# Hybrid attention, Fourier and Hyena block on one core: square sums, filters and modulation loads of the first phase rearranged

## The chip, the core and the metric

The kernel runs on one core of a Trainium2 chip. The metric is the device time of one execution in microseconds (us). In the text PE is TensorE, DVE is VectorE, ACT is ScalarE, and SP is SyncE, which here only issues DMAs. "L157" is line 157 of the kernel before.

## What is computed

One layer of a diffusion backbone over 256 latent tokens and 256 context tokens of width 2048. Cut to what matters here:

```
s_lat, s_ctx = silu(c), silu(c_ctx)
mod   = s_lat @ ada_w + ada_b           # six parts of 2048: sh1, sc1, g1, sh2, sc2, g2
mod_c = s_ctx @ ada_w + ada_b
h  = rmsnorm(x,   norm1_g) * (1 + sc1)  + sh1
hc = rmsnorm(ctx, norm1_g) * (1 + csc1) + csh1
q, k, v, f, hy = split(h @ w_in)
kc, vc = split(hc @ w_in[:, 1024:3072])
a = neighbourhood attention of q over k, v and all of kc, vc
y = concat(rmsnorm(a), rmsnorm(fourier(f)), rmsnorm(hyena(hy, filters)))
x = x + g1 * (y @ w_out)
x = x + g2 * mlp(modulated rmsnorm(x))
return rmsnorm(x)
```

The Hyena filters come from a small network of two sine layers over 256 positions: `hdn = sin(freq * (sin(freq * (z @ w1 + b1)) @ w2 + b2))`, `h = (hdn @ w3) * decay`, with a forward and a backward half for each of two orders. What the later stages need of them is a spectrum of the sum and one of the difference of the two halves; the backward half has no element 0.

## The kernel before

Everything is float32. The large products run as three float32r products (high by high, high by low, low by high; `mm3`, L159), so every weight chunk that arrives is split by ACT (`w_hi`, L168) and DVE (`w_lo`, L169). Products whose operands are plain float32 appear in the trace as two PE instructions each.

**First phase (L344 to L584).** It computes the keys and values of both streams, `kT` and `v_t`. The 16 row tiles of the model width are taken in five blocks of 2, 2, 4, 4 and 4 (`blocks`). A block has four column groups (`group`, L502): two for the keys, in which a latent and a context half follow each other, and two for the values. The first block writes its sums by ACT, the later ones add by DVE (L527).

A block needs its row tiles normalised and modulated, `hprep` (L474). That needs `A1` and `B1`, the modulation columns, which come from `ada_w`: a block of 2 row tiles takes 4 MB of it, one of 4 takes 8 MB, in loads of 512 KB (`ada_load`, L425). `part` (L435) loads all that one of the two halves (scale `m=0`, shift `m=1`) needs, multiplies it with the two silu vectors on PE (L445, four strips of 32 columns side by side), copies the result (L447), transposes it (L165) and reduces it (L451). The two parts of block b+1 are placed in the program before the groups 0 and 2 of block b; those of block 0 (`p0`, `p1`) and of block 1 (`e`, `e`) stand in the start.

**The start** is an order of named steps written out by hand, `start` in `CFG` (L52), each name a step of the dictionary at L545. In the order of the string: constants are loaded (`hp`, `pk`, `h3`, `dc`, `ft`), then the latent tokens (`x0 x1`); `si` is the silu; `w0` to `w3` are PE products whose results nobody reads (`warm`, L376); `n1s`, `n2s` are the sine layers (`sine`, L364); `hw` forms sum and difference of the filter weights on 64 rows (L384); `fr` computes element 0 apart (L388); `f0 f1` are the filters, `s0 s1` their spectra (`fold`, L171). The squares of the tokens (`squares`, L411) are taken by ACT, summed over four row tiles at a time by DVE (L418, `TENSOR_REDUCE`), and the four partial sums are summed over the rows by PE with columns of one element (`rms_bcast`, L197), which then puts the factor on all 128 rows through a diagonal matrix (`dg`, L208). `sr` loads and silus `s_row`, the vector that the side work reads.

**Side work.** Four further modulation vectors are computed by DVE from 128 loads of 512 KB (`ada_col_t`, L308, L309), two per `pump` (L318). `p1` in `CFG` gives the pumps in each block of the first phase.

**What sets the order.** SP issues all loads in the order of the program, and an issue waits until its buffer is free. Weight chunks, `ada_w` loads and side loads share one pool of 8 buffers of 512 KB (`w_raw`). On the other engines the framework orders the instructions when the kernel is built, by the program's order and by its own forecast of when operands are there; on the chip each engine then runs its list in order.

After the first phase come the Fourier and Hyena groups with their projections (L670 to L760), attention with the output projection, and the gated MLP. Nothing of them is touched.

Of the kernel before, what the change touches and what calls it, by code (L numbers as in the profile page):

```python
# [15 lines left out]
P = 128  # L16
D = 2048
# [18 lines left out]
for _n, _k in V_LAYOUT:  # L36
# [10 lines left out]
    p1=(3, 0, 3, 5, 6),  # L47
# [4 lines left out]
    start='hp pk h3 dc ft x0 x1 si w0 n1s w1 n2s hw w2 w3 a00 a01 a10 fr q0 f0 p0 a11 p1 n0 h0 s0 c0 w c1 f1 e s1 q1 n1 h1 sr e',  # L52
    late='',
    warm=(8, 2, 6, 3),
# [70 lines left out]
def hybrid_block(ctx: ExitStack, tc: tile.TileContext, a: dict, out: bass.AP):  # L125
# [71 lines left out]
    def rms_bcast(pool_, sqs, n, name):  # L197
        ps = bank()
        for t in range(2):
            for j, sq in enumerate(sqs):  # L200
                mm(ps[:, t : t + 1], sq[:, t * P : (t + 1) * P], ones[:, 0:1], j == 0, j == len(sqs) - 1)
        ms = pool_.tile([P, 2], F32, name=f"{name}_m", tag=f"{name}_m")
        TS(ms[:], ps[:, 0:2], 1.0 / n, EPS, op0=ALU.mult, op1=ALU.add)
        r = rstd_of(pool_, ms[:], 2, name)
        ps = bank()
        for t in range(2):
            dg = cst.tile([P, P], F32, tag="dg", name="dg", bufs=2)
            TS(dg[:], ident, r[:, t : t + 1], None, op0=ALU.mult)  # L208
# [3 lines left out]
        return rb  # L212

# [13 lines left out]
    class Weights:  # L227
        def __init__(self, stack, nraw, nsp, side=None):
            self.raw = pool(stack, "w_raw", nraw, side)
            self.sp = pool(stack, "w_split", nsp, side)  # L230

        def load(self, src, nk, n):
            r = self.raw.tile([P, nk, n], F32, tag="raw", name="raw")
            nc.sync.dma_start(r[:], src.rearrange("p (k n) -> p k n", n=n))
            return r

        def chunk(self, src, i, nk, n):
            raws = []
            for q in range(2):
                z = (slice(None), slice(q * nk // 2, (q + 1) * nk // 2))  # L240
                raws.append((z, self.load(src[2 * i + q], nk // 2, n)))
            hi = self.sp.tile([P, nk, n], F32R, tag="hi", name="w_hi")
# [86 lines left out]
    c_pool = pool(p1s, "c_lo", 1, "right")  # L329
    s_t = p1.tile([P, KT, 32], F32, name="s_t")  # L330
# [13 lines left out]
    if True:  # L344
        hpack = w1.raw.tile([64, L + 2 * 64 + 3], F32, tag="raw", name="hpack")
        hw3, hwsd = spec[:64, 0], spec[:64, 1]
        tb = v_t[:, :, HYW:]
        decay = tb[:, 0:2, :]
        kz = p1.tile([P, 4, HYW], F32, name="kz")
        hv = hpack[:, 0:3]  # L350
        hw1 = hpack[:33, 3:67]
        hw2 = hpack[:, 67:131]
        zT = hpack[:33, 131 : 131 + L]
        hd1, hd2 = tb[:64, 2, :L], tb[:64, 2, L:]
# [9 lines left out]
        def sine(dst, w, src, b):  # L364
            ps = bank()
            mm(ps[:64, :L], w, src, True, True)
            arg, k = tb[:64, 3, :L], tb[:64, 3, L:]
            TS(arg, ps[:64, :L], hv[:, b : b + 1], hv[:, 2:3], op0=ALU.add, op1=ALU.mult)
# [12 lines left out]
        def sums():  # L381
            for o in range(2):
                for z, op in enumerate((ALU.add, ALU.subtract)):
                    TT(hwsd[:, 2 * o + z, :], hw3[:, 2 * o, :], hw3[:, 2 * o + 1, :], op=op)  # L384

        frow = p1.tile([1, 2, HYW], F32, name="frow")

        def first_row(o):  # L388
            ps = bank()
            mm(ps[0:1, :], hd2[:, 0:1], hw3[:, 2 * o, :], True, True)  # L390
            TT(frow[:, o, :], ps[0:1, :], decay[0:1, 0, :], op=ALU.mult)
# [14 lines left out]
    if True:  # L406
# [4 lines left out]
        def squares(v):  # L411
            parts = []
            for q in range(4):
                pt = v_t[:, q, v * L : (v + 1) * L]
                sq = kT[:, 2 * (q % 2) : 2 * (q % 2) + 2, :].rearrange("p a (b n) -> p a b n", n=L)
                for j in range(2):
                    nc.scalar.activation(sq[:, j], xs[v].tiles[2 * q + j][:], AF.Square)
                nc.vector.tensor_reduce(pt, sq.rearrange("p a b n -> p n (a b)"), axis=AX.X, op=ALU.add)  # L418
                parts.append(pt)
            return parts  # L420

        def normalise(v, parts):
            rbs[v] = rms_bcast(p1, parts, D, f"rs{v}")

        def ada_load(k0, w, m, q):  # L425
            n2 = 2048 // w
            nh = n2 // 2
            return [w1.load(a["ada_t"][ada_at[k0, m, 2 * q + i]], nh, w) for i in range(2)]

        def prep_pieces(k0, nk):  # L430
# [4 lines left out]
            def part(m):  # L435
                raws = []
                for q in range(KT // n2):
                    raws += ada_raw.pop((m, q)) if (m, q) in ada_raw and k0 == 0 else ada_load(k0, w, m, q)
                if m == 0:
                    st_["red"] = p1.tile([P, 2, 4, 2], F32, tag="red", name="red", bufs=2)  # L440
                red = st_["red"]
                ps = bank()
                for kt in range(KT):
                    j = kt % 4
                    nc.tensor.matmul(ps[32 * j : 32 * j + 32, :w], s_t[:, kt, :], raws[kt // (n2 // 2)][:, kt % (n2 // 2), :], start=kt < 4, stop=kt >= KT - 4, skip_group_check=True)  # L445
                sb = p1.tile([P, 512], F32, tag="adasb", name="adasb", bufs=1)
                nc.scalar.copy(sb[:, :w], ps[:, :w])  # L447
                ps = bank()
                for i in range(nk):
                    transpose(ps[:, i * P : (i + 1) * P], sb[:, i * P : (i + 1) * P])  # L450
                nc.vector.tensor_reduce(red[:, m, :nk, :], ps[:, :w].rearrange("p (i j m) -> p i m j", j=4, m=32)[:, :, 0:2, :], axis=AX.X, op=ALU.add)  # L451

            def first():
                part(0)

            def second():
                part(1)
                red = st_["red"]
                for vv in range(2):
                    TT(red[:, 0, :nk, vv], red[:, 0, :nk, vv], vec[:, V_B0 + 16 + k0 : V_B0 + 16 + k0 + nk], op=ALU.add)  # L460
                    STT(A1[:, k0 : k0 + nk, vv], red[:, 0, :nk, vv], 1.0, vec[:, V_N1 + k0 : V_N1 + k0 + nk], op0=ALU.add, op1=ALU.mult)
                    TT(B1[:, k0 : k0 + nk, vv], red[:, 1, :nk, vv], vec[:, V_B0 + k0 : V_B0 + k0 + nk], op=ALU.add)
                if k0 > 0:
                    hprep(k0, nk, 0)
                    hprep(k0, nk, 1)

            return [first, second]
# [62 lines left out]
        pieces = block_pieces(0)  # L530
        parts = {}
        ahead = block_pieces(1)
# [4 lines left out]
        def first_rows():  # L537
            first_row(0)
            first_row(1)

        def sq(v):
            parts[v] = squares(v)

        wn = CFG["warm"]
        steps = {  # L545
            "hp": lambda: nc.sync.dma_start(hpack[:], a["hpack"]),
            "pk": lambda: nc.sync.dma_start(pack[:], a["pack"]),
            "h3": lambda: nc.sync.dma_start(hw3, a["hy_w3"][0].rearrange("k (g n) -> k g n", n=HYW)),
# [3 lines left out]
            "sr": silu_row, "si": silu, "n1s": lambda: sine(hd1, hw1, zT, 0), "n2s": lambda: sine(hd2, hw2, hd1, 1), "hw": sums,  # L552
            "w0": lambda: warm(ones[:], wn[0]), "w1": lambda: warm(decay[:, 0, :], wn[1]),
            "w2": lambda: warm(ftab.rearrange("p a n -> p (a n)"), wn[2]), "w3": lambda: warm(xs[0][:, 0, :], wn[3]),
            "c0": lambda: load_pairs(xs[1], a["cT"], 0), "c1": lambda: load_pairs(xs[1], a["cT"], 1),
            "fr": first_rows, "f0": lambda: filters(0), "f1": lambda: filters(1), "s0": lambda: spectra(0), "s1": lambda: spectra(1),
            "q0": lambda: sq(0), "q1": lambda: sq(1), "n0": lambda: normalise(0, parts[0]), "n1": lambda: normalise(1, parts[1]),
            "a00": lambda: pre_ada(0, 0), "a01": lambda: pre_ada(0, 1), "a10": lambda: pre_ada(1, 0), "a11": lambda: pre_ada(1, 1),
            "p0": pieces[0], "p1": pieces[1],
# [4 lines left out]
        late = CFG["late"].split()  # L564
        for z in CFG["start"].split():
            steps[z]()
        for b in range(len(blocks)):
            todo = (ahead if b == 0 else block_pieces(b + 1)) if b + 1 < len(blocks) else []
            n0 = len(todo)
            budget = 0.0  # L570
            for g in range(4):
# [3 lines left out]
                while late and b == 0:  # L575
                    z = late.pop(0)
                    if z == "|":
                        break
                    steps[z]()
# [319 lines left out]
def laid_out(inp):  # L899
# [28 lines left out]
    h = np.zeros((64, L + 2 * 64 + 3), f32)  # L928
    for i, n in enumerate(("hy_b1", "hy_b2", "hy_freq")):
        h[:, i] = inp[n][0]  # L930
    h[:33, 3:67] = inp["hy_w1"][0]
    h[:, 67:131] = inp["hy_w2"][0]
    h[:33, 131:] = z.T
# [49 lines left out]
```

## Time and profile before

| what | us |
|---|---|
| median of 3 runs (1346.88 to 1348.91) | 1347.93 |
| the profiled execution, whole | 1349.0 |
| its span, first to last instruction | 1347.2 |
| PE busy in the span | 1315.8 |
| DVE busy | 906.1 |
| ACT busy | 555.9 |

The page shows busy time by engine, the span in 40 slices, the DMA queues, the chain of work that ended last, and the costliest groups of instructions. PE's granted clock over the whole span is 0.991. The loads moved 309.35 MB. A row of the windows view has, for one stretch, its length, then busy time and number of instructions of PE, PE's weight loads, DVE, ACT and, where it ran, POOL, and at last the granted PE clock, the busy share of the DMA engines, and GB/s.

### The profile page before, as it was taken

The numbers are of one execution on the slowest core, as the hardware profiler recorded it, in microseconds if no ns is written. First come the engines' busy times: TensorE is split into PE (matmuls) and PEld (weight loads), VectorE is DVE, ScalarE is ACT, GpSimd is POOL, SyncE is SP. The second block draws the span as 40 slices with busy tenths as digits, with TensorE's granted clock in tenths as the row PEclk, the third lists the DMA queues.
The fourth block names the chain that finished last, engine by engine and source line by source line (L and its number), as shares of the span: only waits on it lengthen the run. The fifth ranks groups of instructions, "written<-read, shape, count | busy, mean of one in ns | idle before, by whom it ended". The sixth has DMA issues, their size and how long they took to land.

```text
span 1347.2 us, 24475 instructions
## 1 busy us (share of the span) xinstructions
PE 1315.8 (98%) x10262; PEld 1232.1 (91%) x10262; DVE 906.1 (67%) x1320; ACT 555.9 (41%) x738; POOL 0.9 (0%) x7
## 2 busy tenths in 40 slices
PE   8899999999999999989999999999999999999996
PEld 4486887999989889989999999999999999999996
DVE  5855668957999889976676767644446555654653
ACT  3542313133343665445443444333334444443542
POOL 0000000000000000000000000000000000000000
PEclk9899999999999999989999999999999999999998
DMA  8788687888669865846777777855555555555541
GB/s 321 281 324 304 241 338 291 323 253 286 212 249 330 309 197 180 281 136 211 252 251 247 250 250 239 281 195 186 184 188 184 189 186 189 187 187 187 182 151 63
DMA packets 93039, 313.05 MB, mean 232 GB/s; under 512 B 16000, under 2 KB 16192, under 8 KB 92480
## 3 DMA queue, kind: packets, MB, share of 16 engines
q1 hardware_dynamic: 92928, 311.49, 67.4%
q8 instruction: 80, 1.31, 0.4%
q14 instruction: 31, 0.25, 0.1%
HBM read 309.35 MB, written 2.10 MB: 231 GB/s over the span
## 4 chain that ended last, share of the span: by engine, by line
PE 94%; DVE 3%; ACT 1%; DMA 1%; issue 0%; DVEq 0%; ACTq 0%; POOL 0%; POOLq 0%
PE acc_ps L157 87%; PE mi_ps L157 4%; PE mi_ps L445 2%; PE mi_ps L165 1%; DMA raw<-in_ada_t 1%; DVE raw L309 0%; ACT w_hi L168 0%; DVE w_lo L169 0%; DMA raw<-in_ada_col_t 0%; DVE xr L894 0%; ACT L188 0%; DVE Y L717 0%; ACT kz L176 0%; ACT s_row L362 0%; DVE u L645 0%
## 5 line engine op out<-in xcount | busy, mean ns | idle before, releaser
L169 DVE TENSOR_TENSOR w_lo<-raw,w_hi 128x1024 fp32r<-128x1024 f32 x376 | 447.9, 1220 | 247.2 <-ACT w_hi L168 246.2
L168 ACT CAST w_hi<-raw 128x1024 fp32r<-128x1024 f32 x376 | 380.4, 1048 | 527.4 <-PE acc_ps L157 475.1
L157 PE MATMUL acc_ps<-h_hi,w_hi 128*128 128x256 f32 x1408 | 395.3, 281 | 1.6 <-ACT h_hi L224 1.6
L157 PE MATMUL acc_ps<-h_hi,w_lo 128*128 128x256 f32 x1408 | 395.3, 281 | 0.0
L157 PE MATMUL acc_ps<-h_lo,w_hi 128*128 128x256 f32 x1408 | 395.3, 281 | 0.0
L157 PEld LDWEIGHTS acc_ps<-h_hi,w_hi 128*128 128x128 f32 x1408 | 265.8, 189 | 1.9 <-ACT h_hi L224 1.9
L157 PEld LDWEIGHTS acc_ps<-h_lo,w_hi 128*128 128x128 f32 x1408 | 265.9, 189 | 0.0
L157 PEld LDWEIGHTS acc_ps<-h_hi,w_lo 128*128 128x128 f32 x1408 | 265.8, 189 | 0.0
L157 PE MATMUL acc_ps<-yh,w_hi 128*128 128x256 f32 x704 | 196.9, 280 | 0.0
L157 PE MATMUL acc_ps<-yl,w_hi 128*128 128x256 f32 x704 | 196.8, 280 | 0.0
L157 PE MATMUL acc_ps<-yh,w_lo 128*128 128x256 f32 x704 | 196.5, 279 | 0.0
L309 DVE SCALAR_TENSOR_TENSOR raw<-raw,s_row 128x1024 f32<-128x1024 f32 x128 | 154.1, 1217 | 30.5 <-DMA raw<-in_ada_col_t 30.5
L157 PE MATMUL acc_ps<-hx_hi,w_hi 128*128 128x256 f32 x512 | 145.1, 284 | 0.0
L157 PE MATMUL acc_ps<-hx_lo,w_hi 128*128 128x256 f32 x512 | 144.4, 282 | 0.0
L157 PE MATMUL acc_ps<-hx_hi,w_lo 128*128 128x256 f32 x512 | 144.0, 283 | 0.0
L157 PEld LDWEIGHTS acc_ps<-yh,w_hi 128*128 128x128 f32 x704 | 132.3, 188 | 0.0
L157 PEld LDWEIGHTS acc_ps<-yh,w_lo 128*128 128x128 f32 x704 | 132.1, 188 | 0.0
L157 PEld LDWEIGHTS acc_ps<-yl,w_hi 128*128 128x128 f32 x704 | 131.9, 187 | 0.0
L157 PEld LDWEIGHTS acc_ps<-hx_hi,w_hi 128*128 128x128 f32 x512 | 96.6, 189 | 5.0 <-issue 4.8
L157 PEld LDWEIGHTS acc_ps<-hx_hi,w_lo 128*128 128x128 f32 x512 | 96.2, 188 | 2.9 <-issue 2.9
L157 PEld LDWEIGHTS acc_ps<-hx_lo,w_hi 128*128 128x128 f32 x512 | 96.5, 188 | 0.8 <-issue 0.7
L623 DVE SCALAR_TENSOR_TENSOR xr<-acc_ps,G,xr 128x256 f32<-128x256 f32 x64 | 27.2, 477 | 20.8 <-PE acc_ps L157 20.8
(222 smaller groups left out, 1546.7 us busy)
## 6 DMA issues: line engine op xcount, KB each, us to landing
raw<-in_ffn_t SPq DMA_DIRECT2D x264, 512.0 KB, 4.3
raw<-in_ada_col_t SPq DMA_DIRECT2D x128, 512.0 KB, 4.8
raw<-in_ada_t SPq DMA_DIRECT2D x64, 512.0 KB, 6.5
raw<-in_w_in_t SPq DMA_DIRECT2D x48, 512.0 KB, 5.3
raw<-in_w_kv_t SPq DMA_DIRECT2D x32, 512.0 KB, 4.5
raw<-in_w_out_t SPq DMA_DIRECT2D x32, 512.0 KB, 4.7
x_in<-in_xT SPq DMA_DIRECT2D x8, 256.0 KB, 6.9
x_in<-in_cT SPq DMA_DIRECT2D x8, 256.0 KB, 8.0
```

What stands on the lines that cost most here:

```text
L157: nc.tensor.matmul(ps, lhsT, rhs, start=start, stop=stop, skip_group_check=True)
L165: nc.tensor.transpose(ps, src, ident[:n, :n])
L168: nc.scalar.copy(hi, src)
L169: TT(lo, src, hi.bitcast(F32), op=ALU.subtract)
L309: STT(r, r, 1.0, s_row[:, h * NA : (h + 1) * NA], op0=ALU.mult, op1=ALU.mult, accum_out=sums_[:, f, h : h + 1])
L445: nc.tensor.matmul(ps[32 * j : 32 * j + 32, :w], s_t[:, kt, :], raws[kt // (n2 // 2)][:, kt % (n2 // 2), :], start=kt < 4, stop=kt >= KT - ...
L623: STT(xr[:, c, :], pss[nt // 2][:, (nt % 2) * L : (nt % 2 + 1) * L], cols[:, c : c + 1], xr[:, c, :], op0=ALU.mult, op1=ALU.add)
```

## The change

- **Tokens first, two queues.** `hpack` and `pack` are issued by ACT, the latent tokens are SP's first loads, then `h3 dc ft`, half of block 0's modulation loads (`a00 a01`), the context tokens (`c0 c1`), the first weight chunk (`W`, `load_early`), and the other half (`a10 a11`).
- **Square sums on PE.** ACT squares each tile pair as before; PE sums them over the rows, for the latent tokens with a matrix of ones, so that the sum stands on all rows and the factor is worked out there (`rms_rows`), for the context tokens with columns of one element (`col_sums`).
- **Filters over 128 rows.** The second sine layer is computed twice, on rows 0 to 63 and 64 to 127, so that forward and backward weights stand below each other; sum and difference come from the products themselves, with a copy of the layer whose lower half has the sign turned (`signed`). `sums` and `first_row` go; `kz` moves into a part of `v_t`.
- **Pieces of 1 MB.** `part` becomes `piece`: one product over 1 MB of `ada_w`, 4 pieces for a block of 2 row tiles, 8 for one of 4, spread over the four groups of the block before. Three of eight loads go to a new pool of 3 buffers (`a_raw`). Block 1's pieces move out of the start into block 0.
- **Moved.** `s_row` is loaded and silued in block 1. The pumps are 0, 0, 2, 6, 9 in place of 3, 0, 3, 5, 6. Two kinds of unread products are left (`wm`, 8 of 128 columns; `wp`, 3 of 384).

```diff
-    p1=(3, 0, 3, 5, 6),
+    p1=(0, 0, 2, 6, 9),
-    start='hp pk h3 dc ft x0 x1 si w0 n1s w1 n2s hw w2 w3 a00 a01 a10 fr q0 f0 p0 a11 p1 n0 h0 s0 c0 w c1 f1 e s1 q1 n1 h1 sr e',
-    warm=(8, 2, 6, 3),
+    start='hp pk x0 x1 h3 dc ft a00 a01 c0 c1 W a10 a11 wm si n1s wp n2s q0 n0 f0 s0 f1 s1 e e q1 n1 e e h0 w h1',
+    warm=(8, 3),
...
+    def col_sums(ps, sqs, first=True, last=True):
+        for j, sq in enumerate(sqs):
+            for t in range(2):
+                mm(ps[:, t : t + 1], sq[:, t * P : (t + 1) * P], ones[:, 0:1], first and j + t == 0, last and j == len(sqs) - 1)
...
+    def rms_rows(pool_, ps, n, name):
+        ms = pool_.tile([P, L], F32, name=f"{name}_m", tag="rr_m")
...
+        TS(ms[:], ps, 1.0 / n, EPS, op0=ALU.mult, op1=ALU.add)
+        nc.scalar.activation(s[:], ms[:], AF.Sqrt)
+        nc.vector.reciprocal(r[:], s[:])
+        STT(s[:], r[:], -0.5, ms[:], op0=ALU.mult, op1=ALU.mult)
+        TT(s[:], s[:], r[:], op=ALU.mult)
+        STT(r[:], s[:], 1.5, r[:], op0=ALU.add, op1=ALU.mult)
...
+    a_raw = pool(p1s, "a_raw", 3, "right")
...
+        def signed():
+            nc.vector.memset(hd2[64:128, 0:1], 0.0)
+            TS(hd2n, hd2, sign, None, op0=ALU.mult)
 
         def filters(o):
             for t in range(2):
-                for z in range(2):
+                for z, hd in enumerate((hd2, hd2n)):
                     ps = bank()
-                    mm(ps[:], hd2[:, t::2], hwsd[:, 2 * o + z, :], True, True)
+                    mm(ps[:], hd[:, t::2], w3[:, o, :], True, True)
                     TT(kz[:, 2 * z + t, :], ps[:], decay[:, t, :], op=ALU.mult)
-            for z in range(2):
-                nc.scalar.copy(kz[0:1, 2 * z, :], frow[:, o, :])
...
+            ps = bank(acc_ps)
+            for q in range(KT // 2):
+                sq = kT[:, q, :].rearrange("p (k n) -> p k n", n=L)
+                nc.scalar.activation(sq, xs[v].tiles[q][:], AF.Square)
+                e = q == KT // 2 - 1
+                if v == 0:
+                    for i in range(2):
+                        mm(ps[:, :L], ones[:], sq[:, i], q + i == 0, e and i == 1)
+                else:
+                    col_sums(ps, [sq[:, 0], sq[:, 1]], q == 0, e)
...
-            return [w1.load(a["ada_t"][ada_at[k0, m, 2 * q + i]], nh, w) for i in range(2)]
+            return [w1.load(a["ada_t"][ada_at[k0, m, 2 * q + i]], nh, w, a_raw if (2 * q + i) % 8 in (0, 3, 5) else None) for i in range(2)]
...
+            return [piece(m, q) for m in range(2) for q in range(last_q + 1)]
...
-        ahead = block_pieces(1)
+        ahead = block_pieces(0)
...
-            "hp": lambda: nc.sync.dma_start(hpack[:], a["hpack"]),
-            "pk": lambda: nc.sync.dma_start(pack[:], a["pack"]),
+            "hp": lambda: nc.scalar.dma_start(hpack[:], a["hpack"]),
+            "pk": lambda: nc.scalar.dma_start(pack[:], a["pack"]),
...
-            todo = (ahead if b == 0 else block_pieces(b + 1)) if b + 1 < len(blocks) else []
+            todo = block_pieces(b + 1) if b + 1 < len(blocks) else []
...
+            if b == 1:
+                silu_row()
```

More of the change, by code (lines that the diff above doesn't have):

```diff
@@ L433, in prep_pieces @@
             st_ = {}
[L435 to L465, printed above, removed]
@@ L563, in hybrid_block @@
         }
-        late = CFG["late"].split()
         for z in CFG["start"].split():
@@ L574, in hybrid_block @@
                 group(b, g)
[L575 to L579, printed above, removed]
                 budget += CFG["p1"][b] / 4.0
```

131 lines of the change are left out of this document (76 added, 55 removed).

## The prediction, on record before the changed kernel ran

> **What bounds the kernel now.** I read the windows view first, cut where PE stops pausing, then the chain of work that ended last, then who waited.
>
> ```profile
> PE 1315.8 (98%) x10262; PEld 1232.1 (91%) x10262; DVE 906.1 (67%) x1320; ACT 555.9 (41%) x738; POOL 0.9 (0%) x7
> ...
> 0.00:66.40 66.40, 54.12 (x289) 29.61 (x289) 46.80 (x87) 29.17 (x47) 0.90 (x7) 0.95 0.81 299
> 66.40:276.50 210.10, 210.09 (x1350) 169.94 (x1350) 145.97 (x259) 56.54 (x82) 0.00 (x0) 1.00 0.81 301
> ...
> 0.99 3.78 PE acc_ps L157 x16
> 10.79 11.00 PE acc_ps L157 x22
> 31.83 7.30 DMA raw<-in_ada_t
> 39.55 2.92 PE mi_ps L157 x6
> 66.52 18.77 PE acc_ps L157 x109
> ```
>
> The reader is to see two stretches. Up to 66.4 us, the start, PE is busy 54.12 of 66.4, and 15 us of the chain there (3.78 and 11.00, `acc_ps` at L157 before any weights exist) are unread products. From 66.4 to 276.5, where the first phase ends, PE is busy for all of 210.10 us. Over the whole kernel PE is busy 98%. So whatever PE saves before 66.4 arrives at the end undiminished, as long as the stretch behind stays without a pause; and nothing else is to be had, because nothing after the first phase is touched.
>
> ```profile
> PE mi_ps L157 <- DVE dg L208: 6.1, 2, 5.0
> PE mi_ps L157 <- ACT v_t L374: 3.9, 1, 3.9
> ...
> 30.00:40.00 10.00, 4.47 (x53) 3.41 (x53) 6.07 (x18) 6.33 (x10) 0.00 (x0) 0.83 1.03 402
> 40.00:50.00 10.00, 9.69 (x26) 4.48 (x26) 9.95 (x16) 5.68 (x11) 0.00 (x0) 0.83 0.95 371
> ```
>
> The 12.3 us in which PE idles in the start (66.40 - 54.12) are mostly two waits: 3.9 for the first sine, and 5.0 for `dg`, the token factor, for which DVE had first to sum squares. After that pause the granted clock was 0.83 in two windows of 10 us, so some 6.8 us ran at half.
>
> **The change, part by part.** I compare what PE has to do from t, the moment at which it works on the groups without pause. Of the work before 66.4, two things are still owed at t in the new order: the group products that the old order had fitted in, and block 1's two parts.
>
> ```profile
> 0.00:66.40 66.40, 20.68 (x73) 13.13 (x73) 0.00 (x0) 0.00 (x0) 0.95 0.81 299
> ...
> L157 PE MATMUL acc_ps<-ones 128*128 128x128 f32 x16 | 3.8, 431 | 1.0 <-POOL ones L153 1.0
> L157 PE MATMUL acc_ps<-v_t 128*128 128x512 f32 x4 | 3.8, 1101 | 0.0
> L157 PE MATMUL acc_ps<-ftab 128*128 128x512 f32 x12 | 6.2, 674 | 0.0
> L157 PE MATMUL acc_ps<-x_in 128*128 128x256 f32 x6 | 1.5, 379 | 0.0
> ...
> 190.00:200.00 10.00, 10.00 (x87) 10.00 (x86) 5.77 (x9) 2.00 (x2) 0.00 (x0) 1.00 0.90 355
> 63.47 1.93 PE L445 MATMUL mi_ps<-raw,s_t 128*32 128x256 f32 x32
> 65.95 0.44 PE L165 MATMUL mi_ps<-pack,adasb 128*128 128x128 f32 x2
> ```
>
> The first row is the start again with `acc_ps` products alone: 73, of which the next four rows, all unread, are 38. The other 35 belong to group 0; at 87 in 10 us they are 4.0 us. A part of block 1 is 1.93 + 0.44 = 2.4 us, two are 4.8, with two more piece boundaries 5.0. So the new first phase ends at t + 210.1 + 4.0 + 5.0 = t + 219.1, and the old order is worth t = 57.4.
>
> Now t itself, by PE's work in the order of the new string.
>
> ```profile
> 10.72 3.78 PE L157 MATMUL acc_ps<-v_t 128*128 128x512 f32 x4
> 20.34 1.46 PE L157 MATMUL acc_ps<-x_in 128*128 128x256 f32 x6
> 54.75 3.60 PE L157 MATMUL mi_ps<-kz,ftab 128*128 128x512 f32 x8
> 58.18 1.84 PE L157 MATMUL mi_ps<-ones,v_t 128*128 128x1 f32 x16
> L157 PE MATMUL mi_ps<-hpack 33*64 33x256 f32 x2 | 1.1, 659 | 0.0
> L157 PE MATMUL mi_ps<-spec,v_t 64*1 64x512 f32 x4 | 1.9, 588 | 0.0
> L157 PE MATMUL mi_ps<-ones,v_t 128*128 128x1 f32 x32 | 3.7, 245 | 0.0
> L157 PE MATMUL mi_ps<-dg,ones 128*128 128x128 f32 x8 | 1.9, 374 | 6.1 <-DVE dg L208 6.1
> ```
>
> - `wm`: as before, from 0.99 for 3.78, together 4.8. Two sine products, 1.1 each: 2.2 (64 or 128 output rows, the same 256 columns).
> - `wp`: 6 passes of 384 columns. A pass of 512 took 0.94 at low clock (3.78 in 4) and 0.45 at full (3.60 in 8), so 2.0 to 4.2; I take 3.0. It replaces 11.5 us of unread products (3.8, 6.2, 1.5).
> - Latent squares on PE: 16 products of 256 columns, 32 passes at 1.39 in 6 (from 20.34 to the next start): **7.4 added**. With them go the latent half of the 3.7 us of `ones,v_t` and about half of the 1.9 of `dg`.
> - Context squares: 64 passes of one column, 16 in 1.84: **7.4**, against 1.84 before. Then the diagonal, 0.7.
> - Filters and spectra: 32 passes of 512 columns, 3.60 in 8: 14.4 (half the rows or all of them stream alike). The 1.9 us of element 0 go.
> - Block 0's four pieces: 2 x 2.4 and two boundaries, 5.2.
>
> Sum 4.8 + 2.2 + 3.0 + 7.4 + 7.4 + 0.7 + 14.4 + 5.2 = 45.1. To this comes idle time. Its bounds are 0 and the 12.3 of before, so t lies between 45.1 and 57.4. I take 3.4, for the following reasons.
>
> ```profile
> L418 DVE TENSOR_REDUCE v_t<-kT 128x256 f32<-128x1024 f32 x8 | 15.1, 1919 | 0.0
> L384 DVE TENSOR_TENSOR spec<-spec 64x512 f32<-64x512 f32 x4 | 2.6, 674 | 0.0
> L391 DVE TENSOR_TENSOR frow<-mi_ps,v_t 1x512 f32<-1x512 f32 x2 | 1.4, 679 | 2.0 <-PE mi_ps L157 2.0
> L189 DVE RECIPROCAL rs_r<-rs_s 128x2 f32<-128x2 f32 x2 | 0.3, 156 | 0.2 <-ACT rs_s L188 0.2
> L220 DVE SCALAR_TENSOR_TENSOR ht<-x_in,A,rs_b 128x256 f32<-128x256 f32 x4 | 1.8, 481 | 0.0
> L447 ACT COPY adasb<-mi_ps 128x256 f32<-128x256 f32 x4 | 1.5, 373 | 7.9 <-PE mi_ps L445 7.8
> L224 ACT ACTIVATE hx_hi<-ht,B 128x256 fp32r<-128x256 f32 x2 | 0.9, 504 | 0.0
> ```
>
> DVE loses 19.1 of its 46.8 us, and with them what held up `dg`. It gains four operations of 128x256 (0.48 each by L220) and a reciprocal of that width: no row has one; below is 0.16 (two elements), above the 1.92 of L418 with four times the elements. I take 1 and cost the whole `rms_rows` at nothing, since it is done some 20 us before the last modulation piece; without that cover it is 4. The sine wait of 3.9 is filled by `wp`. What stays is the chain behind the last piece, about 3: copy 0.37, transposes 0.44, reduce and sums about 0.9, then 0.48 and 0.50 for the first modulated tile. PE has the context sums to lay over it only if the framework orders them so.
>
> The loads are early enough. By the sizes, 11.3 MB stand ahead of `a11`'s end; at the 402 of the window quoted above that is about 30 us, well before PE reaches the last pieces. The added wait is that of the fourth `a_raw` load, the last of `a11`: it needs the first piece's buffer, so SP stands there until about 36 us, and behind it are chunk 1 and block 1's first loads. They are wanted after t, 12 us later. The two issues on ACT cost it about 1.2 us while it waits for `pack` anyway, until 5.33.
>
> [...]
>
> In the long stretch little changes: 24 pieces replace 6 parts of which the framework had split several anyway; I take 0, between -2 and +2. At the turn from block 1 to block 2 the last piece is now only one group ahead (48 products, 5.6 us), where two groups stood before, and `hprep` of four tiles takes DVE 4 x 0.96: I take a stall of 1.0, between 0 and 3.
>
> The sum: t = 48.5, end of the phase 48.5 + 219.1 + 1.0 = 268.6 against 276.5, so 7.9 us less. The span becomes 1339.3, the profiled execution 1349.0 - 7.9 = 1341.1; that execution lies 1.1 above the median of the runs, and for the median I predict **1340.0**.
>
> **The rivals.**
>
> *The start keeps its waits* (17%). PE's list is fixed when the kernel is built; if it asks for something before it is there, idle time of 7 to 12 us returns. For: that is how 5.0 us arose at `dg`. Against: the sum on DVE that caused it is gone. Result 1343.6 to 1348.6.
>
> *A pause drops the clock* (7%). After the 7.3 us of the chain's DMA piece the clock was half for 6.8 us. If the chain behind the last piece does this again, up to 3.4 us of work is lost: 1343.4. [...]
>
> *No idle at all* (12%): t = 45.1, no stall at the turn, unsplit pieces 2 us cheaper: 1333.6.
>
> *Block 1 waits for its loads* (8%), the slower side. Block 1's 4 MB no longer come in the start.
>
> ```profile
> 60.00:70.00 10.00, 8.91 (x87) 7.41 (x87) 8.87 (x26) 5.33 (x12) 0.00 (x0) 1.00 0.47 174
> 180.00:190.00 10.00, 10.00 (x87) 9.95 (x86) 8.13 (x16) 2.19 (x3) 0.00 (x0) 1.00 1.02 413
> ```
>
> Between 36 and 100 us chunks 1 to 4, the `ada_w` of blocks 1 and 2 and `s_row` must land: 32 loads of 0.524 MB and 1.05, 17.8 MB in 64 us, 279 GB/s. The long stretch before ran at 301, and 413 has been reached; but with all buffers full it was 174. At 235 the last piece is 12 us late, which takes the gain and 4 us more: 1352. It turns slower below about 248. Against: 11 buffers instead of 8.
>
> **How the numbers follow.** Forecast 56%, the others as given. A measurement of this kernel can tell about 0.2% from no change, 2.7 us: faster is below 1345.2. That holds the forecast, "no idle", "clock" and a third of "keeps its waits": 0.81. Same 0.11, slower 0.08. The range 1333 to 1347 leaves out the load rival and the worst end of the waits.
>
> **What would show it.** Right: no `TENSOR_REDUCE` in the first phase, PE's group products from about 48 us without pause, the last `v_t` add near 268 instead of 276, clock 1.00 from 20 us on. Wrong: idle PE ended by `raw<-in_ada_t` between 70 and 110 us; `dg` or `ht` ending a pause of over 4 us; or side loads that, 18 of them in block 4, push the first `in_w_in_t` chunk behind its use.

## The result: 1340.88 us, and the profile after

| | before | after |
|---|---|---|
| median (lowest to highest), 7 runs each | 1348.86 (1345.88 to 1351.11) | 1340.88 (1336.22 to 1345.28) |
| ratio to before, 95% interval | | 0.9944 (0.9931 to 0.9957) |
| span of the profiled execution | 1347.2 | 1338.5 |

The prediction was 1340.0. Line numbers from here on are those of the changed kernel: `mm` is L156, `piece` L466, its copy L470, `modulate` L239, the adds L547.

The page of the changed kernel, its row of busy times; then the row of the last adds of the first phase, for each kernel (their start times are "first and last start").

```profile
PE 1311.0 (98%) x10302; PEld 1235.1 (92%) x10302; DVE 890.7 (67%) x1305; ACT 555.7 (42%) x735; POOL 0.9 (0%) x7
```

```profile
L527 DVE TENSOR_TENSOR v_t<-acc_ps,v_t x32: 673/680/692, 108.5 to 275.9; 128x512 f32<-128x512 f32 x32
```

```profile
L547 DVE TENSOR_TENSOR v_t<-acc_ps,v_t x32: 683/692/699, 103.4 to 267.3; 128x512 f32<-128x512 f32 x32
```

The whole gain is there when the first phase ends: 275.9 - 267.3 = 8.6 us of the 8.7 by which the spans differ. The stages behind it neither add nor take anything in the sum: from the last add to the end it is 1071.3 us before and 1071.2 after. That is a balance, not a rule. In the other kernels below, none of which touches these stages, the same distance lies between 1070.0 (e2) and 1078.0 (e6).

The windows of the changed kernel, cut where its group products run without pause (columns as in the prediction):

```profile
0.00:55.00 55.00, 47.59 (x232) 30.87 (x232) 25.95 (x60) 21.52 (x37) 0.91 (x7) 0.91 0.78 274
55.00:268.80 213.80, 213.80 (x1447) 173.03 (x1448) 150.27 (x267) 61.28 (x89) 0.00 (x0) 0.99 0.84 315
```

The point t is 55.0, not 48.5. The long stretch takes 213.8, not 220.1. Two errors of 6.5 and 6.3 us cancel: the sum was hit by chance, its two main terms were not. The start shows why it is late: PE idles 55.0 - 47.6 = 7.4 us, and the granted clock (the share of full speed that PE was given, 1.00 at best) is 0.91 on the average. Windows of 2 us show when it falls.

```profile
38.00:40.00 2.00, 2.00 (x20) 2.00 (x20) 0.00 (x0) 0.00 (x0) 0.00 (x0) 1.00 1.18 266
40.00:42.00 2.00, 2.00 (x16) 2.00 (x17) 0.00 (x0) 0.00 (x0) 0.00 (x0) 0.81 0.86 352
42.00:44.00 2.00, 2.00 (x11) 2.00 (x12) 0.00 (x0) 0.00 (x0) 0.00 (x0) 0.50 1.02 416
44.00:46.00 2.00, 0.62 (x3) 0.22 (x3) 1.87 (x11) 0.20 (x1) 0.00 (x0) 0.50 0.63 256
46.00:48.00 2.00, 0.71 (x3) 0.74 (x4) 1.34 (x7) 0.00 (x0) 0.00 (x0) 0.50 0.02 6
48.00:50.00 2.00, 2.00 (x19) 0.98 (x21) 0.42 (x1) 0.00 (x0) 0.00 (x0) 0.50 0.03 8
50.00:52.00 2.00, 1.83 (x20) 0.59 (x12) 0.00 (x0) 0.04 (x1) 0.00 (x0) 0.63 0.62 182
52.00:54.00 2.00, 0.61 (x3) 0.37 (x4) 1.09 (x4) 2.00 (x4) 0.00 (x0) 1.00 0.65 193
```

The order of the rows matters. PE is busy for every microsecond of 38 to 44, and the clock falls to half inside that time; the pause comes after, at 44. A pause can't be its cause. What PE does there, by its timeline and by the groups of the start (0 to 55 us):

```profile
34.29 1.93 PE L466 MATMUL mi_ps<-raw,s_t 128*32 128x256 f32 x32
36.16 7.94 PE L156 MATMUL acc_ps<-ones,kT 128*128 128x1 f32 x58
43.96 0.67 PE L164 MATMUL mi_ps<-pack,adasb 128*128 128x128 f32 x2
47.29 1.20 PE L156 MATMUL mi_ps<-dg,ones 128*128 128x128 f32 x4 [2.66 <-DVE dg L211]
48.41 3.42 PE L466 MATMUL mi_ps<-raw,s_t 128*32 128x256 f32 x32
```

```profile
L156 PE MATMUL acc_ps<-ones,kT 128*128 128x1 f32 x64 | 8.7, 269 | 0.0
L156 PE MATMUL mi_ps<-v_t,ftab 128*128 128x512 f32 x16 | 7.4, 604 | 1.3 <-DVE v_t L417 1.3
L156 PE MATMUL acc_ps<-kT,ones 128*128 128x256 f32 x32 | 7.3, 382 | 0.0
L156 PE MATMUL mi_ps<-spec,v_t 128*128 128x512 f32 x16 | 7.2, 593 | 0.0
```

The products at 36.16 are the context squares, the products of one column. Pieces of the same size took 1.93 at 34.29 and take 3.42 at 48.41. What the low clock cost is the busy time of a window times what is missing of the clock: 0.38 + 1.0 + 0.31 + 0.36 + 1.0 + 0.68 = 3.7 us between 40 and 52. A second spell costs 5.71 x 0.28 = 1.6 more:

```profile
54.00:60.00 6.00, 5.71 (x38) 3.92 (x39) 4.15 (x8) 2.03 (x4) 0.00 (x0) 0.72 1.01 394
```

This one does stand behind a pause: from 52 to 54 PE is busy for 0.61 of 2.00.

So two questions go to the chip: whether the one-column products drop the clock, or the pause at `dg` does in some way; and which parts of the change carry the gain.

### The profile page after: what moved, and what is told of

Same layout as the page of the kernel before. It is cut to its first block, busy times and chain, and to the rows that moved or that the text cites. A ratio compares the mean times of both kernels' runs of the same rounds, so it can differ in the third digit from the quotient of the medians.

```text
span 1338.5 us, 24519 instructions
## 1 busy us (share of the span) xinstructions
PE 1311.0 (98%) x10302; PEld 1235.1 (92%) x10302; DVE 890.7 (67%) x1305; ACT 555.7 (42%) x735; POOL 0.9 (0%) x7
## 4 chain that ended last, share of the span: by engine, by line
PE 94%; DVE 3%; DMA 1%; ACT 1%; issue 0%; DVEq 0%; ACTq 0%
PE acc_ps L156 87%; PE mi_ps L156 4%; PE mi_ps L466 2%; PE mi_ps L164 1%; DMA raw<-in_ada_col_t 1%; DVE w_lo L168 0%; DMA pack<-in_pack 0%; DVE xr L908 0%; ACT w_hi L167 0%; DVE raw L333 0%; DVE Y L731 0%; DVE rs_r L223 0%; ACT PT L825 0%; DVE u L659 0%; DVE gt L666 0%
## 5 line engine op out<-in xcount | busy, mean ns | idle before, releaser
L156 PE MATMUL acc_ps<-h_hi,w_hi 128*128 128x256 f32 x1408 | 394.7, 281 | 1.6 <-ACT h_hi L239 1.6
L156 PE MATMUL acc_ps<-h_lo,w_hi 128*128 128x256 f32 x1408 | 394.7, 280 | 0.0
L156 PE MATMUL acc_ps<-h_hi,w_lo 128*128 128x256 f32 x1408 | 394.7, 280 | 0.0
L156 PEld LDWEIGHTS acc_ps<-h_hi,w_hi 128*128 128x128 f32 x1408 | 265.7, 189 | 1.8 <-ACT h_hi L239 1.8
L156 PEld LDWEIGHTS acc_ps<-h_lo,w_hi 128*128 128x128 f32 x1408 | 265.7, 189 | 0.0
L156 PEld LDWEIGHTS acc_ps<-h_hi,w_lo 128*128 128x128 f32 x1408 | 265.7, 189 | 0.0
L156 PE MATMUL acc_ps<-yh,w_lo 128*128 128x256 f32 x704 | 196.8, 280 | 0.0
L156 PE MATMUL acc_ps<-yl,w_hi 128*128 128x256 f32 x704 | 196.7, 279 | 0.0
L156 PE MATMUL acc_ps<-yh,w_hi 128*128 128x256 f32 x704 | 196.4, 279 | 0.0
L156 PE MATMUL acc_ps<-hx_hi,w_hi 128*128 128x256 f32 x512 | 145.0, 285 | 1.0 <-ACT hx_hi L239 1.0
L156 PE MATMUL acc_ps<-hx_lo,w_hi 128*128 128x256 f32 x512 | 144.8, 283 | 0.3 <-DVE hx_lo L240 0.3
L156 PE MATMUL acc_ps<-hx_hi,w_lo 128*128 128x256 f32 x512 | 144.0, 283 | 0.0
L156 PEld LDWEIGHTS acc_ps<-yl,w_hi 128*128 128x128 f32 x704 | 132.3, 188 | 0.0
L156 PEld LDWEIGHTS acc_ps<-yh,w_hi 128*128 128x128 f32 x704 | 132.0, 187 | 0.0
L156 PEld LDWEIGHTS acc_ps<-yh,w_lo 128*128 128x128 f32 x704 | 131.9, 187 | 0.0
L156 PEld LDWEIGHTS acc_ps<-hx_hi,w_hi 128*128 128x128 f32 x512 | 96.5, 189 | 6.6 <-ACT w_hi L167 2.5
L156 PEld LDWEIGHTS acc_ps<-hx_lo,w_hi 128*128 128x128 f32 x512 | 97.0, 190 | 1.5 <-issue 0.9
L156 PEld LDWEIGHTS acc_ps<-hx_hi,w_lo 128*128 128x128 f32 x512 | 96.7, 189 | 1.5 <-issue 1.5
```

The source lines that it names most:

```text
L156: nc.tensor.matmul(ps, lhsT, rhs, start=start, stop=stop, skip_group_check=True)
```

## The experiments

Each of these kernels was timed in five rounds beside the kernel before, whose median lay between 1347.9 and 1349.2 in them; kernels are therefore best compared by the ratio. "Last add" is the start of the last `v_t` add in the one profiled execution.

| kernel | median us (runs) | ratio, 95% interval | last add |
|---|---|---|---|
| the changed kernel | 1340.88 (7) | 0.9944 (0.9931 to 0.9957) | 267.3 |
| e1_wide_sums | 1338.20 (6) | 0.9928 (0.9906 to 0.9950) | 261.8 |
| e2_rows_both | 1332.05 (4) | 0.9882 (0.9864 to 0.9900) | 261.2 |
| e3_before_pe_sums | 1352.26 (12) | 1.0026 (1.0012 to 1.0040) | 280.7 |
| e10_before_rows | 1345.84 (12) | 0.9983 (0.9969 to 0.9997) | 272.0 |
| e4_dve_sums | 1348.78 (12) | 1.0002 (0.9990 to 1.0014) | 274.0 |
| e5_bursts | 1345.84 (12) | 0.9982 (0.9966 to 0.9997) | 269.5 |
| e8_pumps | 1351.36 (12) | 1.0020 (1.0007 to 1.0033) | 274.2 |
| e6_no_araw | 1343.87 (12) | 0.9967 (0.9951 to 0.9983) | 265.7 |
| e7_load_order | 1343.53 (12) | 0.9959 (0.9945 to 0.9974) | 270.2 |
| e9_no_unread | 1340.56 (6) | 0.9935 (0.9911 to 0.9958) | 270.3 |
| e11_rows_no_unread | 1332.55 (5) | 0.9888 (0.9869 to 0.9907) | 260.3 |

### What drops the clock

**e1_wide_sums**: the changed kernel, each context sum with 128 equal columns of ones in place of one (`wd` is 128); same number of products, same order in the program.

```diff
-    mm(ps[:, t : t + 1], sq[:, t * P : (t + 1) * P], ones[:, 0:1], ...)
+    mm(ps[:, t * wd : t * wd + wd], sq[:, t * P : (t + 1) * P], ones[:, 0:wd], ...)
-        TS(ms[:], ps[:, 0:2], 1.0 / n, EPS, ...)
+        TS(ms[:], ps[:, 0 : 2 * wd : wd], 1.0 / n, EPS, ...)
```

> The changed kernel with one edit: the 64 passes that sum the context squares on PE have 128 equal columns of ones in place of one; they take the same 0.11 us each and feed the same operations. Theory C (one-column products do not hold the clock): in the changed kernel the clock fell to half at about 41 us, in the middle of these passes and before any pause; here it stays 1.00 from 12 to 60 us, the pieces behind take 1.9 us and not 3.4, and the time falls by 3 to 4 us to about 1337. Rival N (the pause of 2.7 us before the diagonal products did it, or the passes themselves are the cost): half clock is there as before, the time stays within 1 us of 1340.9.

Its timeline of PE, then its windows:

```profile
36.78 6.42 PE L156 MATMUL acc_ps<-ones,kT 128*128 128x128 f32 x56
...
46.69 0.68 PE L156 MATMUL mi_ps<-dg,ones 128*128 128x128 f32 x4 [3.49 <-DVE dg L211]
```

```profile
40.00:42.00 2.00, 2.00 (x20) 2.00 (x19) 0.00 (x0) 1.04 (x1) 0.00 (x0) 1.00 1.03 399
42.00:44.00 2.00, 1.20 (x11) 1.00 (x9) 0.77 (x2) 0.57 (x2) 0.00 (x0) 1.00 1.01 412
44.00:46.00 2.00, 0.00 (x0) 0.00 (x0) 1.93 (x5) 0.56 (x1) 0.00 (x0) 1.00 1.01 416
```

128 times the columns, and the passes are not dearer but cheaper (56 in 6.42 against 58 in 7.94), as the clock stays at 1.00 from 20 to 70 us; beside both, PE's weight loads are busy all the time (PEld 2.00 of 2.00 from 38 to 44 us in the changed kernel, from 36 to 42 here). The pause at `dg` is even longer, 3.49 us, and drops nothing. So the single columns were the cause of the spell that begins at 41 us, the pause was not. The other kernels bear it out: between 40 and 50 us the clock is 0.50 to 0.57 in all seven profiles with the 64 one-column products (the changed kernel, e3, e5 to e9), and 0.86 to 1.00 in the four without (e1, e2, e10, e11). The phase ends 5.5 us earlier in the profiles, where the low clock had been priced at 3.7 + 1.6 = 5.3. By medians the gain is only 2.7, with intervals that overlap: the profiled execution, at 1333.9, was the fastest of this kernel's six. e1 decides by the clock, not by the time.

**e2_rows_both**: the context summed as the latent tokens are, by a matrix of ones with 256 columns; `dg` goes too.

```diff
-                if v == 0:
-                    for i in range(2):
-                        mm(ps[:, :L], ones[:], sq[:, i], ...)
-                else:
-                    col_sums(ps, [sq[:, 0], sq[:, 1]], q == 0, e)
+                for i in range(2):
+                    mm(ps[:, :L], ones[:], sq[:, i], ...)
...
-            rbs[v] = rms_bcast(p1, None, D, f"rs{v}", ps) if v else rms_rows(p1, ps[:, :L], D, f"rs{v}")
+            rbs[v] = rms_rows(p1, ps[:, :L], D, f"rs{v}")
```

> The changed kernel with the context squares summed like the latent ones, by a matrix of ones (32 passes of 256 columns), the factor worked out on all 128 rows by DVE; the diagonal products go. Theory C: clock 1.00 throughout the start, the wait of 2.7 us and the 1.2 us of the diagonal go too, first group products near 49 us, time 5 to 8 us below the changed kernel: 1333 to 1336. Rival N: only the wait and the diagonal go, about 3.5 us: 1337 to 1338. Rival D (DVE, with 3.7 us more of work on 256 columns, holds up the second half of group 0): no gain, 1340 to 1342.

```profile
40.00:50.00 10.00, 8.82 (x82) 5.61 (x81) 5.87 (x11) 3.68 (x6) 0.00 (x0) 1.00 0.92 342
50.00:60.00 10.00, 9.80 (x84) 9.18 (x85) 3.66 (x13) 3.63 (x7) 0.00 (x0) 1.00 1.02 390
```

The windows show the clock at 1.00 and there is no wait for `dg`. 1332.05 us is 8.8 below the changed kernel, with intervals that stand apart: this version beats both kernels. The first group product comes at 48.5, where the prediction had put t. Theory C holds in each of its signs, and the time is 1 us below its range.

**e3_before_pe_sums** and **e10_before_rows** do the same on the kernel before: e3 takes the change's two kinds of sums on PE and nothing else, and PE then has no pause where the clock falls; e10 is e3 with the matrix of ones for both streams (the diff of e2).

> The kernel before with the square sums of both streams on PE as in the changed kernel, and nothing else of the change. Theory S (the square sums are the gain): the wait of 5.0 us for dg goes, most of the gain is here, 1340 to 1343. Rival W (PE pays 11 us more for the sums than it did, which only the rest of the rearrangement earns back): wait 5.0 gone, PE 11 us more, no gain: 1347 to 1353.

> The kernel before with the square sums of both streams on PE by the matrix of ones (as e2 has them), and nothing else of the change. With one-column sums for the context (e3) the clock was half for 13.7 us though PE had no pause from 10 to 69 us. Theory C: that half clock goes, 5 to 8 us below e3's 1352.3: 1344 to 1347, so the square sums alone are worth a little. Rival W (PE's 11 us of added work is the loss in e3): 1350 to 1353.

The windows of e3, then of e10:

```profile
40.00:50.00 10.00, 10.00 (x64) 7.49 (x63) 1.44 (x7) 0.37 (x1) 0.00 (x0) 0.51 0.87 326
50.00:60.00 10.00, 10.00 (x27) 5.01 (x27) 8.85 (x17) 4.90 (x8) 0.00 (x0) 0.81 0.58 196
```

```profile
40.00:50.00 10.00, 10.00 (x39) 4.95 (x41) 8.98 (x14) 4.97 (x8) 0.00 (x0) 1.00 1.01 408
50.00:60.00 10.00, 10.00 (x83) 5.81 (x75) 4.64 (x12) 6.50 (x8) 0.00 (x0) 1.00 1.00 381
```

e3 is the cleanest case: PE is busy 20.00 of 20.00, not one pause, and the clock is at half for 2 x (4.9 + 1.9) = 13.6 us. Half of it, 6.8, is lost work; e10, without the one-column products, has none of it and is 0.43% or 5.8 us faster by the ratios. In e3 alone this turns a small gain into a loss of 3.5 us. By its time e3 lies in the range of rival W, which put the loss down to PE's added work; e10 has that work too and does not lose, so W's reason is wrong.

### Which parts carry the gain

**e4_dve_sums**: the changed kernel with the squares summed by DVE, as before (in tiles of their own).

> The changed kernel with the square sums back on DVE as before (reduce over four tiles, then 16 one-column passes), all else as changed. Theory S: the waits on DVE come back, 15 us of reduces stand before the filters' multiplies, and the gain is lost: 1345 to 1350. Rival W: PE has 11 us less to do, the loads come early, DVE has room (26 of 55 us busy in the changed start), and the clock may fall in a pause: 1336 to 1342.

```profile
PE mi_ps L156 <- DVE dg L211: 8.2, 2, 4.9
PE mi_ps L156 <- ACT v_t L401: 5.2, 1, 5.2
```

```profile
20.00:30.00 10.00, 6.10 (x12) 3.13 (x12) 5.35 (x18) 2.42 (x4) 0.00 (x0) 0.50 1.04 399
```

Nothing is left of the gain, as theory S had it: PE waits 8.2 us for `dg` and 5.2 for the sine, and works at half clock around them (0.67 in the window of 10 us before this row). The two halves don't add. By the ratios, sums on PE by the matrix of ones alone gain 0.2% (e10), the rest alone nothing (e4, 1.0002), and both together 1.2% (e2).

**e8_pumps**: the side work nearly as before.

```diff
-    p1=(0, 0, 2, 6, 9),
+    p1=(0, 3, 3, 5, 6),
```

> The changed kernel with the side work spread over the first phase nearly as before (0, 3, 3, 5, 6 pumps instead of 0, 0, 2, 6, 9). Theory L (early loads are short, so side loads must stand late): 6 loads of 0.5 MB in block 1 and 2 more in block 2 delay block 1's and block 2's own loads by up to 4 MB at about 300 GB/s, 13 us; with what slack there is, PE pauses of 1 to 6 us ended by a raw tile between 60 and 120 us, 1342 to 1347. Theory H (slack): no pause, 1339 to 1342; and the wait for X in the Hyena stage, 3.3 us against 2.3 before, unchanged or 1 us shorter as fewer side loads stand at the end of the phase.

By its median this was the dearest single edit, 10.5 us (its interval overlaps that of e4), and slower than both theories: L, with pauses alone, ended at 1347. The chain of waits and the timeline at the turn from block 1 to block 2:

```profile
111.51 1.01 PE mi_ps L466 x4
...
112.91 4.15 DMA raw<-in_ada_t
...
117.24 0.52 ACT hx_hi L239
```

```profile
106.75 1.05 PE L466 MATMUL mi_ps<-raw,s_t 128*32 128x512 f32 x4
...
117.80 1.23 PE L156 MATMUL acc_ps<-hx_hi,w_hi 128*128 128x256 f32 x4 [2.04 <-ACT hx_hi L239]
```

A modulation load lands late behind the side loads (4.15 us in the chain), the last piece is late, and PE pauses 2.04 us for the first modulated tile of block 2. The larger part is less visible: PE stays busy, but pieces are cut into runs of 4 products, eight such runs in e8. One takes 1.05, where the changed kernel has 16 in one run:

```profile
99.80 1.92 PE L466 MATMUL mi_ps<-raw,s_t 128*32 128x512 f32 x16
```

That is 0.48 for four, so a run of four costs some 0.6 us more (an estimate from these two rows). A run of 8 in the kernel before takes hardly more than one of 4, 1.06 (at 118.41). In the run of 16 a product takes 0.12 (1.92 in 16), while a pass of 512 columns of the filters takes 0.45 (3.60 in 8), so it goes at the pace of about four at once, and a run of 4 at that of about two (1.05 in 4, or 0.26 each); these are estimates from the rows, and why a run of 4 is slower was not tested. The pieces alone in the long stretch (the windows view for the instructions on `s_t`), in the order before, changed, e8, e5:

```profile
66.40:276.50 210.10, 26.68 (x192) 6.03 (x192) 0.00 (x0) 0.00 (x0) 1.00 0.81 301
```

```profile
55.00:268.80 213.80, 28.01 (x256) 6.62 (x256) 0.00 (x0) 0.00 (x0) 0.99 0.84 315
```

```profile
53.40:275.60 222.20, 33.02 (x256) 6.94 (x256) 0.00 (x0) 0.00 (x0) 0.99 0.84 309
```

```profile
55.00:271.10 216.10, 31.11 (x256) 7.37 (x256) 0.00 (x0) 0.00 (x0) 1.00 0.84 311
```

The same 256 products take 28.0 us in the changed kernel and 33.0 in e8. Of the 8.4 us that e8's stretch is longer (222.2 - 213.8), 5.0 are the pieces and 2.4 pauses (PE is busy 219.84 of 222.20). That is not the whole loss: the last add is 6.9 later than in the changed kernel, the end of the span 11.0. The 4.1 behind the phase stood in neither theory. Part of it is the clock: behind the wait for `X` in the Hyena stage it is at half for 6.9 us (0.61 and 0.53 in the windows of 4 us from 400 to 408), in the changed kernel for 3.4 (0.57 from 396 to 400). The rest was not followed.

**e5_bursts**: pieces in two bursts per block, before groups 0 and 2, as the parts had stood.

```diff
-                while todo and n0 - len(todo) < n0 * (g + 1) / 4:
+                while todo and n0 - len(todo) < n0 * (g // 2 + 1) / 2:
```

> The changed kernel with the pieces of the next block placed as the parts were before, half of them ahead of group 0 and half ahead of group 2. Theory P (the spreading is part of the gain): loads of 4 MB wait for buffers in bursts, PE pauses or splits products between 55 and 210 us, 2 to 6 us above the changed kernel: 1343 to 1347. Rival Q (the long stretch was without pauses before too, the gain is all in the start): within 1.5 us of 1340.9.

The pieces cost 31.11 against 28.01, and the last add is 2.2 later; PE has no pause in the stretch. So of the two ways that theory P named, pauses and split products, it is the second: the cut pieces again. Of the 5.0 us by medians the other half arises later. In the profile 2.6 us of it lie behind the last add, and the Hyena stage accounts for 1.7 of them: PE waits 4.2 us in all for `X` against 3.3, and behind that wait the clock is at half for 6.8 us in place of 3.4, which costs 2.5 us of work against 1.7. The rest was not followed.

**e6_no_araw** takes away the extra pool of 3 buffers; **e7_load_order** has the old order of the first loads, all issued by SP; **e9_no_unread** leaves out both kinds of unread products.

```diff
-    a_raw = pool(p1s, "a_raw", 3, "right")
-            return [w1.load(..., a_raw if (2 * q + i) % 8 in (0, 3, 5) else None) for i in range(2)]
+            return [w1.load(...) for i in range(2)]
```

```diff
-    start='hp pk x0 x1 h3 dc ft a00 ...
+    start='hp pk h3 dc ft x0 x1 a00 ...
-            "hp": lambda: nc.scalar.dma_start(hpack[:], a["hpack"]),
+            "hp": lambda: nc.sync.dma_start(hpack[:], a["hpack"]),
...
```

```diff
-    ... a10 a11 wm si n1s wp n2s q0 ...
+    ... a10 a11 si n1s n2s q0 ...
```

> The changed kernel without the extra pool of 3 buffers for the modulation loads: all loads share the 8 buffers again. Theory L (the rival 'block 1 waits for its loads' had a real price, which the 11 buffers removed): the loads of block 0's last pieces must wait until a first piece is done (at 36 us in the changed kernel), land 5 us after that, and the block 1 loads behind them come as much later; PE pauses ended by a raw tile appear in the start or between 60 and 110 us, 3 to 8 us together, time 1344 to 1349. Theory H (loads have slack; the 64 context passes from 36 to 44 us and the later weight chunks cover it): no pause ended by a raw tile over 1 us, 1339 to 1342, same as the changed kernel.

> The changed kernel with the first loads in the old order (constants, then tokens) and all on SP. Theory O (tokens first is part of the gain): the last token tile lands near 15 us instead of 11, PE stands with its list at the latent sums, 2 to 5 us above the changed kernel: 1343 to 1346. Rival Q (the sine layers end at 16 us in both and the modulation pieces are no later): within 1.5 us of 1340.9.

> The changed kernel without its two kinds of unread products (wm and wp). Theory W (they hold the clock): the latent sums start at half clock, their 32 passes take up to 0.43 us each instead of 0.22, 2 to 6 us above the changed kernel: 1343 to 1347. Rival F (PE waits for tokens and sines anyway, and 6.5 us of unread work go): from 2 us below to 1 us above 1340.9.

e6: no load was late in the first phase, whose last add came even earlier, at 265.7. What it lost, it lost in the stage behind (waits from 280 to 400 us, e6 first, then the changed kernel):

```profile
PE mi_ps L156 <- DVE X L737: 3.8, 1, 3.8
PE acc_ps L156 <- DVE w_lo L168: 2.1, 4, 1.3
```

```profile
PE mi_ps L156 <- DVE X L738: 3.3, 1, 3.3
```

Theory H held for the phase, and the total of 3.0 us more (the intervals just overlap) was foreseen by neither: the time is next to theory L's range, but the late loads that L named are not there. e7 lost 2.7 by medians, with intervals that overlap, so that the loss is not clear of the noise; it has waits for the tokens and for the sine that the changed kernel does not have:

```profile
PE acc_ps L156 <- ACT kT L432: 1.9, 1, 1.9
...
PE mi_ps L156 <- ACT v_t L401: 1.3, 1, 1.3
```

e9 made no measurable difference: PE waits 5.1 us for `hpack` instead of doing unread work, and the 32 passes of the latent sums take 12.1 us in place of 7.3, the first ten some 0.5 each against 0.23. So the slow passes that theory W named do come, though the clock column is 1.00 there (0 to 20 us), and they use up what was saved (the latent sums end at 19.8 us, against 18.4 with the unread products); the time is that of rival F.

**e11_rows_no_unread**: e2 without the unread products, to ask the same where no one-column products are in the way.

> The changed kernel with the context squares summed as the latent ones are (matrix of ones, 256 columns, no one-column products) and without the two kinds of unread products, wm and wp. Leaving out the unread products alone gave no measurable change, but there the one-column products still dropped the clock. Theory W (the unread products keep the clock up, which pays once nothing else drops it): PE pauses while it waits for the tokens and the sine, the granted clock is at half for 3 to 7 us in the first 20 us, and what is saved (4.8 and 4.0 us of unread work) is lost again: 1331 to 1334, as with them. Theory F (pure cost): group products start up to 4 us earlier than 48.5 and the time is 1328 to 1331.

```profile
PE mi_ps L156 <- DMA hpack<-in_hpack: 4.9, 1, 4.9
PE acc_ps L156 <- ACT hx_hi L239: 1.8, 1, 1.8
```

The last add is 0.9 us earlier, the time the same as e2's within the intervals. The number is theory W's. Of its reason only a part is there: the latent sums start slowly (the first four passes 0.52 each, from 11.19 us on 0.23), but the first group product still comes at 45.9, 2.6 us before that of e2. The larger part is lost behind it, in the pause for `hx_hi` and a clock of 0.86 between 40 and 50, which falls after that pause, at 46 to 48. Unread products are not needed here, and do no harm.

## Why the prediction was right, and where it was right by chance

The bound was read rightly: PE had no pause from t to the end of the phase, and the end of the phase decided, 8.6 of 8.7 us. The amount was forecast at 7.9. That it came out so is luck, as these steps show:

- **t = 48.5, measured 55.0.** The 4.8 for `wm` hold 0.99 of waiting, so the sum had 44.1 of work and 4.4 of idle time. Measured are 47.6 and 7.4: the work was 3.5 too small, the idle time 3.0. The large terms of work hold at full clock: filters and spectra 14.4 (7.4 + 7.2), latent squares 7.4 (7.3). That half the rows take about as long as all of them holds as well: in e10, 8 passes of 512 columns took 3.71 on 64 rows and 3.60 on 128. The low clock added 3.7, so without it the work would have been 43.9. `wp` took 4.2 (6 passes at 0.69) where 3.0 was taken.
- **"The sum on DVE that caused it is gone"**: the pause at `dg` stayed, 2.66 us instead of 5.0. The wide reduction had gone, but for the context the factor still went through a diagonal, and DVE had a split of 1.2 us and two modulations ahead of it.
- **`rms_rows` at nothing**, "some 20 us before the last modulation piece": true for the modulation, wrong for what stands beside it in DVE's list. Its reciprocal took 1.74 (1 was taken) and stood between two filter multiplies, for whose result PE waited 1.27. The rows, from DVE's timeline and from PE's:

```profile
20.77 1.74 DVE L223 RECIPROCAL rs_r<-rs_s 128x256 f32<-128x256 f32 x1
22.43 0.63 DVE L417 TENSOR_TENSOR v_t<-mi_ps,v_t 128x512 f32<-128x512 f32 x1
```

```profile
23.11 3.70 PE L156 MATMUL mi_ps<-v_t,ftab 128*128 128x512 f32 x8 [1.27 <-DVE v_t L417]
```

- **The rival "the start keeps its waits"** (17%) nearly came true: its idle time of 7 to 12 us counts as the sum does, and by that count 6.4 came, 2.66 of it at `dg`. Its time of 1343.6 or more did not, because the long stretch was shorter.
- **The rival "a pause drops the clock"** (7%) foresaw up to 3.4 us of lost work, and 5.3 were lost. For 3.7 of it the cause was another: products that keep PE busy (e1, e3, e10). The prediction had costed the context squares by their time alone. For the 1.6 behind the pause at 52 us the rival may be right; no run separates it. The 7.3 us that it took for the pause are a load in the chain; PE's own pause there was 5.0.
- **The long stretch, 219.1 + 1.0, measured 213.8.** The pieces alone were forecast at 26.7 + 2 x 1.93 = 30.5 and took 28.0: 2.5 less. The term "I take 0, between -2 and +2" was mis-sized: what a short run costs was not seen, though the trace before had such runs. The turn cost 0 instead of 1.0. Of the other 2.8, 1.2 are group products (183.8 + 4.0 forecast, 186.6 measured); the rest was not followed.
- **"Block 1 waits for its loads"** (8%) did not occur, and e8 shows that the mechanism was real and what kept it away: not the 11 buffers (e6 has 8, and no such wait), but the pumps, moved to later blocks. The prediction's 17.8 MB leave side loads out without a word on what they would cost; with 3 pumps in block 1 and a third one in block 2 the whole gain is gone.
- **`hpack` beside the tokens.** With ACT as its issuer and 2 MB of tokens issued by SP at the same time, `hpack` landed 4.4 us after its issue, against 2.6 in e7, where SP issues it ahead of everything. The delay of 1.8 us is less than the 5 that 2 MB take at the 402 GB/s of the window from 30 to 40 us before (an estimate). PE waited 0.4 us for `hpack`, with `wm` ahead; without `wm` it waits 4.9 to 5.1 (e11, e9) and the time is the same.

Of the marks set beforehand, the last add (near 268, measured 267.3) and the missing wide `TENSOR_REDUCE` were right; the group products from 48 and the clock of 1.00 from 20 us on were wrong. e2, which has neither the spell of half clock nor `dg`, shows both.

Not settled: where e2 loses most of its early start (its first group product is 3.1 us ahead of e1's, its last add only 0.6); why the wait for `X` in the Hyena stage differs between kernels (2.3 before, 3.3 after, 2.7 in e2, 3.7 in e5), and what makes up for it in the changed kernel, where the clock is at half for 3.4 us behind that wait and in the kernel before it is not; what part of the gain the filters over 128 rows and the pieces of 1 MB carry by themselves, as no run takes them alone.

## What to carry to other kernels

Sum over rows with a matrix of ones and many columns rather than with columns of one element: at full clock PE needs about the same time for both (32 passes in 7.3 us, or 64 at 1.84 for 16, which makes 7.4), the wide form needs no second product to spread the result, and it kept the clock (1.00 from 40 to 50 us in e2 and e10, 0.56 in the changed kernel and 0.51 in e3). When a profile shows a busy PE, read the granted clock and the number of products beside it: neither half clock (e3: 0.51 with PE busy 10.00 of 10.00) nor cut runs of small products (e8: 33.0 us for what took 28.0) appear as idle time. And when side work moves, count its loads against the loads that it would stand in front of; here that was worth as much as the whole gain (e8: 10.5 us by the medians).

## What the runs showed of the hardware

**A busy PE can lose its clock.** In the changed kernel the clock fell between 40 and 42 us, some 5 us after the one-column products began at 36.16 (in e3 some 4 after 36.21), with no pause before (PE busy 2.00 of 2.00 in each window of 2 us from 36 to 44, in e3 to 56). The time at half by the windows is 2 x (0.38 + 4.0 + 0.74) = 10.2 us, in e3 13.6. What the clock goes by is not shown: it is not PE's busy time in the trace, and no run tried widths between 1 and 128 columns.

**One pause does not decide.** 3.49 us without a product (e1) left the clock at 1.00. A wait of 1.8 us in e11, which has no one-column products, was followed by 2 x (0.38 + 1.0 + 0.34) = 3.4 us at half (0.81, 0.50 and 0.83 in the windows of 2 us from 46 to 52). After 2.04 us at 116 in e8 it was at half for 2 x (1.2 + 0.6) = 3.6 us by the windows below, and 3.4 by windows of 2 us (0.90, 0.50 and 0.75 from 116 to 122):

```profile
100.00:120.00 20.00, 17.64 (x72) 9.72 (x70) 14.01 (x25) 1.86 (x4) 0.00 (x0) 0.94 0.92 327
120.00:140.00 20.00, 20.00 (x146) 14.62 (x143) 10.34 (x24) 6.69 (x11) 0.00 (x0) 0.97 0.62 206
```

**Half the pace at the start, with the clock column at 1.00.** The column is 1.00 in the first 10 us of the changed kernel, but the passes of `wm`, 128 columns wide, took 0.24 each (3.78 in 16), where those of e1 took 0.11 (6.42 in 56), and the passes of `wp` 0.69 for 384 columns, where those of the filters took 0.45 for 512. PE ran at about half its later pace, and the column does not show why. The same holds for the 0.94 that the prediction calls low clock: it is read from the pace, the column is 1.00.

**Reciprocal.** 128 x 256 elements took DVE 1.74 us, four times the 0.42 of a multiply of that size.
